# Moving a precomputed weight combination of a seven-product encoder layer from its merge to its first projections, and giving paired weight loads a second set of buffers

## The chip, the cores and the metric

The kernel is one program on one core of one Trainium2 chip. A core has TensorE for matmuls (PE in the profile, with its weight loads as PEld), VectorE (DVE), ScalarE (ACT), GpSimd (POOL) and SyncE (SP). SP computes nothing here: it issues most of the DMA transfers. Every engine works through its own queue in order, and waits on semaphores for the others. The metric is the device time of one execution in microseconds (us).

## The reference

One layer of an encoder runs over two sequences, 256 and 1024 tokens of width 1024, in float32. The kernel treats them as 1280 tokens, that is ten tiles of 128. Cut to its stages:

```
h      = rms_norm(x);  proj = h @ w_in                     # z, conv channels, gates, q, k, v, ...
b0..b3 = ssd_mixer, pool_mixer, sgu_mixer, gla_mixer       # four branches, 512 wide
merged = sum_n sigmoid(gate_n) * (b_n @ w_branch[n])       # "the merge"
x      = x + rms_norm(merged @ w_out)
hidden = relu(rms_norm(x) @ w_ff1) ** 2                    # first product, 1024 to 4096
out    = x + rms_norm(hidden @ w_ff2)                      # second product, 4096 to 1024
```

The SSD mixer comes first. Its input, 768 channels, goes through a depthwise convolution over five tokens and a SiLU before its scans.

## The kernel before, in words

**Numbers.** Each float32 operand is split into a high and a low part (`whi` and `wlo` for weights), and a product takes three passes (high-high, high-low, low-high) at 128x128 weights by up to 512 columns. For a weight block of 128x512 (256 KB) this takes a load into a buffer `raw`, a copy by ACT to `whi` and a subtraction by DVE to `wlo` (`wload`, L129 to L137). There are three buffers of the tag `raw` and sixteen of the tag `w`.

**Seven products in place of eight.** Some of the gate projections and most of both feed-forward products use a scheme of the Strassen-Winograd kind: a 2x2 block product is made with seven block products over sums and differences of blocks. On the weights' side these are T1 = B12 - B11, T2 = B22 - T1, T3 = B22 - B12 and T4 = B21 - T2. For the second product the seven are done one after another (`SECOND`), each over 5 pairs of token tiles and 4 groups of 4 weight blocks. Before product i+1 needs its 16 weight blocks, they are loaded and split while product i runs (`ff2_w`, L1351 to L1367). The right sides T1, T3 and T4 need two blocks each (`RIGHT`): both are loaded into buffers of the tag `raw`, and one DVE subtraction (L1360) makes the difference in the first of them. T4 takes T2 as its second block.

**T2 made ahead.** T2 of the second product needs three blocks and is used twice (as itself and in T4). It is therefore made once, in 16 pieces of 128x512, and kept in DRAM (`t2d`). In the kernel before this happens during the merge: `t2_in(q)` loads B12, B11 and B22 of piece q through POOL's DMA queue (L1093, the tiles named `B` in the profile) and `t2_out(q)` makes two DVE subtractions (L1098, L1099) and stores the piece through POOL's queue (L1100). The buffers are a pool of their own, two of each of the three. The code allows a new piece from step 3 of the merge's 32 steps on, one every 13/8 steps, so the last one at step 27, counted from 0; a piece goes out one step after it came in.

**The merge** (L1103 to L1134) takes 32 steps, eight blocks of 128 output channels for each of four branches, in the order 0, 2, 1, 3. A step makes three products (256, 512 and 512 tokens, each 12 matmuls, L1125) in four PSUM banks of the tag `mm`. DVE takes each out of PSUM: for the first branch one operation (L1130, into `merged`), for the others two (L1132, L1133). `branch` (L1064 to L1073) loads the four 128x1280 pieces of a branch (`bt`) and splits them by ACT (L1071) and DVE (L1072), the first branch through POOL's DMA queue, the others through SP's. Each step also needs one gate tile (`gate`, 640 KB) and one weight block.

**The front.** After the input norm and transposes, PE makes the z projection (L172, to about 77 us), the small `misc` projection and the six projections of the SSD mixer's channels (`conv_gemm`, L453 to L463, 94 to 183 us), each three chunks of 256, 512 and 512 tokens with 24 matmuls. The convolution of each, on DVE, takes one operation (L549), four (L552), a tanh by ACT (L554) and one more (L555), all 1284 elements wide. Then PE runs 11 us of other projections (`fill(11)`; `fill` puts in pieces of later projections) before it transposes the convolved channels (`token_major`, L585). `chunk_state` and the loop behind it use tiles `sx`, `xst` and `rtmp` of the pool `sv`.

**What sets the order.** From the SSD stage on, PE's order is that of the code (`manual_schedule` for PE). The other engines' queues, those of the DMA issuers too, are ordered by a scheduler when the program is built, so an instruction can stand in its queue well ahead of its place in the code. An engine never leaves that order at run time. A tile waits for the last use of the memory that it takes over.

Of the kernel before, what the change touches and what calls it, by code (L numbers as in the profile page):

```python
# [8 lines left out]
F32 = mybir.dt.float32  # L9
# [3 lines left out]
ALU = mybir.AluOpType  # L13
# [9 lines left out]
DFF = 4096  # L23
# [53 lines left out]
FF2_U = FF1_U + 64  # L77
# [4 lines left out]
def encoder_kernel(ctx, tc, x, wu, small, rows, w2, sguw, poolw, consts, y):  # L82
    nc = tc.nc
    PS = bass.MemoryType.PSUM
    PE, ACT, DVE, POOL, SP = nc.tensor, nc.scalar, nc.vector, nc.gpsimd, nc.sync

    def pool(name, bufs=1, **kw):
        return tc.alloc_tile_pool(name=name, bufs=bufs, reuse_waits="tile", **kw)

    dram = ctx.enter_context(tc.tile_pool(name="dram", bufs=1, space=bass.MemoryType.DRAM))  # L90
    cp = pool("const")
    wp = pool("w")
# [4 lines left out]
    def mm_ps():  # L97
        return pmm.tile([128, 512], F32, tag="mm", name="mm", bufs=4)
# [62 lines left out]
    def gemm_a(ps, w, act, c, n):  # L161
        j, last = 0, 3 * w.nk - 1
        for k in range(w.nk):
            for a, b in PASSES:
                PE.matmul(ps[:, :n], w.get(a, k), act.rhs(b, k, c), start=j == 0, stop=j == last)
                j += 1
# [83 lines left out]
    def ts():  # L250
        return tp.tile([128, 512], F32, tag="ts", name="ts", bufs=3)
# [104 lines left out]
    def scratch(name, n):  # L356
        return [dram.tile([128, 512], F32, name=f"{name}{i}") for i in range(n)]
# [22 lines left out]
    def gelu2(ps, n):  # L380

        a = ev1("ga")
        ACT.activation(out=a[:, :n], in_=ps[:, :n], func=AF.Square, scale=float(np.sqrt(0.044715)))
        DVE.scalar_tensor_tensor(out=a[:, :n], in0=a[:, :n], scalar=1.0, in1=ps[:, :n], op0=ALU.add, op1=ALU.mult)
        ACT.activation(out=a[:, :n], in_=a[:, :n], func=AF.Tanh, scale=float(np.sqrt(2.0 / np.pi)))
        DVE.scalar_tensor_tensor(out=a[:, :n], in0=a[:, :n], scalar=1.0, in1=ps[:, :n], op0=ALU.add, op1=ALU.mult)
        return a
# [21 lines left out]
    for g in range(4):  # L409
        tasks.append((stream_a, WA, SU_U + 2 * g, lambda ps, c, c0, n, d=sud[g]: SP.dma_start(  # L410
            out=d[:, c0:c0 + n], in_=gelu2(ps, n)[:, :n])))
    for n_b in EARLY:
        for q in range(8):
            tasks.append((stream_a, WA, GATE_U + 16 * n_b + 2 * q, lambda ps, c, c0, n, d=gtd[n_b][q]: ACT.dma_start(
                out=d[:, c0:c0 + n], in_=tanh_half(ps, n)[:, :n])))
# [13 lines left out]
    def fill(us):  # L429

        while us > 0:
# [2 lines left out]
                return  # L434
            us -= cost

    w = WB(Z_U, 8, given=zw)
    for t in range(NT):
        ps = mm_ps()
# [11 lines left out]
    sv = pool("sv")  # L451

    def conv_gemm(i):  # L453
        w = WA(XBC_U + 2 * i, 8)
        pad = sv.tile([128, NTOK + 8], F32, name="pad", bufs=2)
        for a, b in ((0, 2), (258, 262), (1286, 1288)):
            POOL.memset(pad[:, a:b], 0.0)
        for c, (c0, n) in enumerate(CH):
            ps = mm_ps()
            gemm_a(ps, w, hT, c, n)  # L460
            o = 2 + c0 if c == 0 else 6 + c0
            ACT.copy(out=pad[:, o:o + n], in_=ps[:, :n])
        return pad  # L463
# [24 lines left out]
    for d in range(2):  # L488
        DVE.tensor_tensor(out=dtx[:, d], in0=tp[:, :160].rearrange("p (t e h) -> p e t h", t=NT, e=2)[:, d],
                          in1=smv("dt_bias")[:, 8 * d:8 * d + 8].unsqueeze(1).to_broadcast([128, NT, 8]), op=ALU.add)  # L490
# [13 lines left out]
    for d in range(2):  # L504
        DVE.scalar_tensor_tensor(out=dtx[:, d], in0=dt[:, d], scalar=-1.0,
                                 in1=ea[:, 8 * d:8 * d + 8].unsqueeze(1).to_broadcast([128, NT, 8]),
# [14 lines left out]
    for g in range(2):  # L521
        ACT.activation(out=dec[64 * g:64 * g + 64].rearrange("p d t h -> p (d t) h"),
                       in_=ps[64 * g:64 * g + 64, 160:320].rearrange("p (q h) -> p q h", h=8)[:, :, 4 * g:4 * g + 4],
# [53 lines left out]
    def v4(a):  # L577
        return a.rearrange("p (h q) -> p h q", h=4)

    xsd = scratch("xsd", NT)  # L580

    def token_major(t):
# [494 lines left out]
        SP.dma_start(out=th, in_=gtd[n][d])  # L1077
        return th


    t2p = pool("t2", side="right")
    t2d = [dram.tile([128, 512], F32, name=f"t2d{q}") for q in range(DFF // 256)]

    def w2_block(b, q):
        if b == "T2":
            return t2d[q]
        return wu[FF2_U + 2 * (2 * q + int(b[1]) - 1) + int(b[2]) - 1]

    def t2_in(q):
        r = []  # L1090
        for b in ("B12", "B11", "B22"):
            r.append(t2p.tile([128, 512], F32, tag=b, name=b, bufs=2))
            POOL.dma_start(out=r[-1], in_=w2_block(b, q))  # L1093
        return r

    def t2_out(q, r):
        b12, b11, b22 = r
        DVE.tensor_tensor(out=b12, in0=b12, in1=b11, op=ALU.subtract)  # L1098
        DVE.tensor_tensor(out=b22, in0=b22, in1=b12, op=ALU.subtract)  # L1099
        POOL.dma_start(out=t2d[q], in_=b22)  # L1100

    t2q = []
    MERGE = [(n, d) for n in ORDER for d in range(8)]  # L1103
    br = branch(ORDER[0], POOL, CH)
    wb = WA(BR_U + 8 * MERGE[0][0] + MERGE[0][1], 4)
# [1 line left out]
    for i, (n_b, d) in enumerate(MERGE):  # L1107
        if i + 1 < len(MERGE):
            nwb = WA(BR_U + 8 * MERGE[i + 1][0] + MERGE[i + 1][1], 4)
        if i + 2 < len(MERGE):  # L1110
            ths.append(gate_in(*MERGE[i + 2]))
        if d == 0 and i:
            br = branch(n_b, SP, ((0, NTOK),))
        if t2q and t2q[-1] is not None:
            t2_out(len(t2q) - 1, t2q[-1])
            t2q[-1] = None
        if len(t2q) < DFF // 256 and i >= 3 + len(t2q) * 13 // 8:
            t2q.append(t2_in(len(t2q)))
        th = ths.pop(0)
        for c, (c0, n) in enumerate(CH):  # L1120
            ps = mm_ps()
            j = 0
            for k in range(4):
                for a, b in PASSES:
                    PE.matmul(ps[:, :n], wb.get(a, k), br[b][k][:, c0:c0 + n], start=j == 0, stop=j == 11)  # L1125
                    j += 1
            dst = merged[:, d, c0:c0 + n]
            t = th[:, c0:c0 + n]
            if i < 8:
                DVE.scalar_tensor_tensor(out=dst, in0=t, scalar=1.0, in1=ps[:, :n], op0=ALU.add, op1=ALU.mult)  # L1130
            else:
                DVE.scalar_tensor_tensor(out=t, in0=t, scalar=1.0, in1=ps[:, :n], op0=ALU.add, op1=ALU.mult)  # L1132
                DVE.tensor_tensor(out=dst, in0=dst, in1=t, op=ALU.add)  # L1133
        wb = nwb  # L1134
    gt.release()
    t2p.release()


    tp = pool("tp")
# [1 line left out]
    op = pool("op", side="right")  # L1141
# [209 lines left out]
    def ff2_w(i, upto):  # L1351

        while len(ws[i]) < upto:
            g, k = divmod(len(ws[i]), 4)
            raw = []
            for b in RIGHT[SECOND[i][1]]:
                raw.append(wp.tile([128, 512], F32, tag="raw", name="raw", bufs=3))
                SP.dma_start(out=raw[-1], in_=w2_block(b, 4 * GO[g] + k))
            if len(raw) > 1:
                DVE.tensor_tensor(out=raw[0], in0=raw[0], in1=raw[1], op=ALU.subtract)  # L1360
            place = (NG * i + g) % 7
            pl, tag, n = (w2p, "w2", 16) if place < 2 else (wp, "w", 16) if place < 4 else (w3p, "w3", 24)
            hi = pl.tile([128, 512], F32R, tag=tag, name="whi", bufs=n)
            lo = pl.tile([128, 512], F32R, tag=tag, name="wlo", bufs=n)
            ACT.copy(out=hi, in_=raw[0])  # L1365
            DVE.tensor_tensor(out=lo, in0=raw[0], in1=hi.bitcast(F32), op=ALU.subtract)  # L1366
            ws[i].append((hi, lo))  # L1367
# [187 lines left out]
```

## Time and profile before

| | us |
|---|---|
| median of three timed runs | 2244.68 |
| their range | 2243.88 to 2245.01 |
| the profiled execution's own time | 2240.51 |
| its span | 2238.4 |
| PE busy | 2171.2 |
| DVE busy | 1389.2 |
| ACT busy | 883.2 |
| POOL busy | 99.6 |

The profile is of one execution. Its span runs from the first to the last instruction; the 2.1 us between span and time lie around it. Busy time counts what an engine does, not what it waits for. Matmuls overlap in the profile (each row's duration holds its pipeline), so the number of matmuls in a stretch says more of PE's pace than its busy time. A row of the timeline has start and duration in us, engine, line, operation, the tile written and the tiles read, how many, and in brackets the idle time before it and what ended that. A row of the waits has who waited for whom, then the total in us, how often, and the longest. A row of the windows has the stretch and its length, then each engine's busy time with its number of instructions, the granted TensorE clock, the busy share of the DMA engines and their GB/s.

### The profile page before, as it was taken

Reading aid. Unit: us, or ns where it says so; the run is one execution under the profiler, and the core shown is the slowest. Engines: PE = TensorE matmul, PEld = TensorE weight load, DVE = VectorE, ACT = ScalarE, POOL = GpSimd, SP = SyncE. Lnnn points to the kernel's source line nnn. Section 1 sums busy time; section 2 is a strip of 40 time slices with the busy share of each in tenths; the row PEclk is TensorE's granted clock in tenths of the full one; section 3 lists DMA queues with packets and bytes.
Section 4 is the critical chain, followed back from the end, with each engine's and each line's share of the span. In section 5 each row is a group of like instructions: output and inputs, shape, how many; then the busy total and the mean of one; then the engine's idle time right before and its main releaser. Section 6 shows DMA issues by size and latency. Waiting matters only on the chain. (4 is left out here: it accounts for less than half of the span.)

```text
span 2238.4 us, 33108 instructions
## 1 busy us (share of the span) xinstructions
PE 2171.2 (97%) x12160; PEld 1917.7 (86%) x12160; DVE 1389.2 (62%) x2374; ACT 883.2 (39%) x1811; POOL 99.6 (4%) x194
## 2 busy tenths in 40 slices
PE   8999999999999999998889999999999999999998
PEld 6887888878888999997668877899999998888776
DVE  6365489677668744444466556576666684466574
ACT  5323787334333444444111124443333354333342
POOL 1000000000010000001310001000000000000000
PEclk9999999999999999998899999999999999999998
DMA  5212465545257333336885322655445577577684
GB/s 184 80 33 102 153 230 168 171 138 164 86 177 223 95 94 93 104 96 197 304 305 179 133 92 100 214 148 150 124 133 151 163 228 227 175 223 234 200 275 136
DMA packets 274866, 362.77 MB, mean 162 GB/s; under 512 B 21616, under 2 KB 160272, under 8 KB 274704
## 3 DMA queue, kind: packets, MB, share of 16 engines
q1 hardware_dynamic: 259216, 325.52, 46.7%
q0 software_dynamic: 5696, 19.40, 2.5%
q10 hardware_dynamic: 9792, 15.73, 2.0%
q8 instruction: 95, 1.56, 0.3%
q14 instruction: 67, 0.55, 0.1%
HBM read 250.92 MB, written 109.66 MB: 161 GB/s over the span
## 5 line engine op out<-in xcount | busy, mean ns | idle before, releaser
L345 PE MATMUL mm<-hT,whi 128*128 128x512 f32 (+1 forms) x960 | 261.6, 361 | 0.0
L1125 PE MATMUL mm<-bt,whi 128*128 128x512 f32 (+1 forms) x768 | 212.8, 365 | 29.2 <-DVE merged L1130 17.4
L1433 PE MATMUL mm<-whi,hidh 128*128 128x512 f32 x560 | 219.4, 392 | 2.5 <-ACT whi L1365 2.5
L1433 PE MATMUL mm<-whi,hidl 128*128 128x512 f32 x560 | 219.3, 392 | 1.9 <-DVE hidl L1375 1.9
L1433 PE MATMUL mm<-wlo,hidh 128*128 128x512 f32 x560 | 219.0, 391 | 0.6 <-DVE wlo L1366 0.6
L135 ACT CAST whi<-raw 128x512 fp32r<-128x512 f32 x142 | 87.1, 620 | 261.3 <-PE mm L1125 171.6
L345 PEld LDWEIGHTS mm<-hT,whi 128*128 128x128 f32 x960 | 166.9, 189 | 26.4 <-issue 3.3
L1125 PEld LDWEIGHTS mm<-bt,whi 128*128 128x128 f32 x768 | 139.3, 194 | 56.1 <-DVE merged L1130 20.2
L345 PE MATMUL mm<-hT,wlo 128*128 128x512 f32 (+1 forms) x480 | 170.3, 355 | 0.0
L311 PE MATMUL mx<-S,whi 128*128 128x256 f32 (+1 forms) x768 | 166.2, 308 | 0.0
L311 PE MATMUL mm<-S,whi 128*128 128x384 f32 (+1 forms) x704 | 157.5, 313 | 2.3 <-ACT fc L315 2.3
L352 PE MATMUL mm<-whi,hT 128*128 128x512 f32 x480 | 152.2, 398 | 0.0
L1125 PE MATMUL mm<-bt,wlo 128*128 128x512 f32 (+1 forms) x384 | 138.3, 360 | 0.0
L136 DVE TENSOR_TENSOR wlo<-raw,whi 128x512 fp32r<-128x512 f32 x142 | 97.0, 687 | 65.6 <-ACT whi L135 65.1
L1365 ACT CAST whi<-raw 128x512 fp32r<-128x512 f32 x112 | 69.1, 621 | 166.7 <-DVE raw L1360 112.9
L268 ACT CAST whi<-ts 128x512 fp32r<-128x512 f32 x112 | 69.2, 621 | 161.3 <-PE mm L311 78.7
L311 PEld LDWEIGHTS mx<-S,whi 128*128 128x128 f32 x768 | 128.8, 189 | 0.0
L1433 PEld LDWEIGHTS mm<-whi,hidh 128*128 128x128 f32 x560 | 105.8, 189 | 25.6 <-ACT whi L1365 3.3
L1433 PEld LDWEIGHTS mm<-whi,hidl 128*128 128x128 f32 x560 | 105.8, 189 | 25.2 <-DVE hidl L1375 3.5
L269 DVE TENSOR_TENSOR wlo<-ts,whi 128x512 fp32r<-128x512 f32 x112 | 77.1, 689 | 80.6 <-ACT whi L268 80.4
L1433 PEld LDWEIGHTS mm<-wlo,hidh 128*128 128x128 f32 x560 | 105.6, 189 | 23.0 <-DVE wlo L1366 1.2
L311 PE MATMUL mm<-hT,whi 128*128 128x256 f32 (+1 forms) x576 | 124.7, 308 | 0.0
(331 smaller groups left out, 4899.1 us busy)
## 6 DMA issues: line engine op xcount, KB each, us to landing
raw<-in_wu_dram SPq DMA_DIRECT2D x362, 256.0 KB, 3.0
gate<-gtd SPq DMA_DIRECT2D x32, 640.0 KB, 4.9
hraw<-hidS SPq DMA_DIRECT2D x80, 256.0 KB, 3.2
hraw<-hidA SPq DMA_DIRECT2D x60, 256.0 KB, 3.3
B<-in_wu_dram POOLq DMA_DIRECT2D x48, 256.0 KB, 5.4
hidS<-fc SPq DMA_DIRECT2D x64, 192.0 KB, 3.2
E<-acsd SPq DMA_DIRECT2D x20, 512.0 KB, 4.7
br<-bo SPq DMA_DIRECT2D x36, 256.0 KB, 3.0
```

Of the source, the lines that this page charges most:

```text
L135: ACT.copy(out=hi, in_=raw)
L136: DVE.tensor_tensor(out=lo, in0=raw, in1=hi.bitcast(F32), op=ALU.subtract)
L268: ACT.copy(out=hi, in_=a)
L269: DVE.tensor_tensor(out=lo, in0=a, in1=hi.bitcast(F32), op=ALU.subtract)
L311: PE.matmul(ps, w[ro][a][:, 128 * k:128 * k + 128], left(lo, p, k, c), start=first and j == 0, stop=j == 11, skip_group_check=not first)
L345: yield from halves(ps, w, n, lambda ps, w, a, b, k, st, sp: PE.matmul(ps[:, :n], w.get(a, k), hT.rhs(b, k, c), start=st, stop=sp))
L352: yield from halves(ps, w, 512, lambda ps, w, a, b, k, st, sp: PE.matmul(ps, hT.lhs(b, k, t), w.get(a, k), start=st, stop=sp))
L1125: PE.matmul(ps[:, :n], wb.get(a, k), br[b][k][:, c0:c0 + n], start=j == 0, stop=j == 11)
L1365: ACT.copy(out=hi, in_=raw[0])
L1433: PE.matmul(ps, h[b][:, 128 * k:128 * k + 128], ws[i][4 * g + k][a], start=g == 0 and k == 0 and (a, b) == (0, 0), stop=g == NG - 1 and k ...
```

## The change

- The making of T2 moves to the front. `t2_step` is called after each of the 18 chunks of `conv_gemm`: it finishes the piece that is loaded and begins the next one, so 17 calls make all 16. A loop ahead of `token_major` would finish what is left.
- Its loads and stores go through SP's queue instead of POOL's.
- Its buffers are now tiles of the pool `sv` that are used only later: `sx` for B12 (one buffer), `rtmp` for B11 (one, now 128x512 wide) and `xst` for B22 (two). The pool `t2` is gone.
- In `ff2_w`, the second block of T1, T3 and T4 is loaded into a buffer of the tag `ts` (three of them, which are idle in the second product); the first stays in `raw`.

The operations of T2, their sizes and their number are the same as before.

```diff
+    def t2_in(q):
+        r = []
+        for b, tag in (("B12", "sx"), ("B11", "rtmp"), ("B22", "xst")):
+            r.append(sv.tile([128, 512], F32, tag=tag, name=tag, bufs=2 if tag == "xst" else 1))
+            SP.dma_start(out=r[-1], in_=w2_block(b, q))
+        return r
+
+    def t2_out(q, r):
+        b12, b11, b22 = r
+        DVE.tensor_tensor(out=b12, in0=b12, in1=b11, op=ALU.subtract)
+        DVE.tensor_tensor(out=b22, in0=b22, in1=b12, op=ALU.subtract)
+        SP.dma_start(out=t2d[q], in_=b22)
+
+    def t2_step():
+        if t2q and t2q[-1] is not None:
+            t2_out(len(t2q) - 1, t2q[-1])
+            t2q[-1] = None
+        if len(t2q) < DFF // 256:
+            t2q.append(t2_in(len(t2q)))
...
             gemm_a(ps, w, hT, c, n)
+            t2_step()
             o = 2 + c0 if c == 0 else 6 + c0
...
+    while len(t2q) < DFF // 256 or t2q[-1] is not None:
+        t2_step()
     xsd = scratch("xsd", NT)
...
-    t2p = pool("t2", side="right")
...
-            r.append(t2p.tile([128, 512], F32, tag=b, name=b, bufs=2))
-            POOL.dma_start(out=r[-1], in_=w2_block(b, q))
...
-        POOL.dma_start(out=t2d[q], in_=b22)
...
-        if t2q and t2q[-1] is not None:
-            t2_out(len(t2q) - 1, t2q[-1])
-            t2q[-1] = None
-        if len(t2q) < DFF // 256 and i >= 3 + len(t2q) * 13 // 8:
-            t2q.append(t2_in(len(t2q)))
...
             for b in RIGHT[SECOND[i][1]]:
-                raw.append(wp.tile([128, 512], F32, tag="raw", name="raw", bufs=3))
+                raw.append(ts() if raw else wp.tile([128, 512], F32, tag="raw", name="raw", bufs=3))
                 SP.dma_start(out=raw[-1], in_=w2_block(b, 4 * GO[g] + k))
```

More of the change, by code (lines that the diff above doesn't have):

```diff
@@ L435, in fill, with w2_block @@
             us -= cost
+    t2d = [dram.tile([128, 512], F32, name=f"t2d{q}") for q in range(DFF // 256)]
+    def w2_block(b, q):
+        if b == "T2":
+            return t2d[q]
+        return wu[FF2_U + 2 * (2 * q + int(b[1]) - 1) + int(b[2]) - 1]
+    def t2_in(q):
[9 more added lines that the diff above has]
+        SP.dma_start(out=t2d[q], in_=b22)
+    t2q = []
+    def t2_step():
[4 more added lines that the diff above has]
+            t2q.append(t2_in(len(t2q)))
     w = WB(Z_U, 8, given=zw)
@@ L1078, in gate_in @@
         return th
-    t2p = pool("t2", side="right")
[L1082 to L1091, printed above, removed]
-            r.append(t2p.tile([128, 512], F32, tag=b, name=b, bufs=2))
[L1093 to L1102, printed above, removed]
     MERGE = [(n, d) for n in ORDER for d in range(8)]
@@ L1135, in encoder_kernel @@
     gt.release()
-    t2p.release()
     tp = pool("tp")
```

## The prediction

> **What bounds the kernel now.** I read the page first, then who waits for whom on PE, then windows of the stages in which PE waits.
>
> ```profile
> span 2238.4 us, 33108 instructions
> PE 2171.2 (97%) x12160; PEld 1917.7 (86%) x12160; DVE 1389.2 (62%) x2374; ACT 883.2 (39%) x1811; POOL 99.6 (4%) x194
> PEclk9999999999999999998899999999999999999998
> ```
>
> PE is the bound: 97% of the span, and its clock is down only in slices 19, 20 and the last. So work moved on other engines counts only where PE waits.
>
> ```profile
> PE mm L1125 <- DVE merged L1130: 17.4, 10, 3.3
> PE mm L1125 <- ACT bt L1071: 10.7, 4, 7.1
> ...
> PE mm L1433 <- ACT whi L1365: 2.5, 2, 2.1
> ```
>
> The largest waits are those of the merge (L1125): for DVE to take a product out of PSUM, and at the start for the first branch's tiles. The second product (L1433) waits little. Busy time understates the loss, because a matmul at a lower clock counts as busy. I count matmuls instead:
>
> ```profile
> core 0: us, PE busy (x) PEld busy (x) DVE busy (x) ACT busy (x) POOL busy (x), PEclk, DMA share, GB/s
> 1045.50:1061.20 15.70, 5.01 (x15) 3.26 (x14) 8.79 (x15) 6.79 (x14) 3.99 (x8) 0.66 1.02 371
> 1061.20:1080.00 18.80, 15.48 (x59) 12.39 (x59) 8.80 (x13) 5.48 (x5) 3.85 (x9) 0.77 0.95 369
> 1080.00:1155.00 75.00, 60.28 (x289) 48.90 (x289) 39.36 (x63) 8.67 (x11) 25.41 (x47) 0.97 0.84 294
> 1155.00:1170.00 15.00, 14.49 (x75) 12.14 (x74) 13.73 (x22) 2.41 (x3) 0.00 (x0) 1.00 0.90 306
> 1170.00:1300.00 130.00, 130.00 (x681) 112.00 (x680) 82.49 (x138) 17.58 (x24) 0.00 (x0) 1.00 0.43 149
> ```
>
> From 1170 us on PE is never idle: 130 / 681 = 0.191 us per matmul. At that pace the four stretches before would take 2.9, 11.3, 55.2 and 14.3 us. They lose 12.8, 7.5, 19.8 and 0.7 us, together 40.8. POOL is busy in the first three only, and POOL does nothing there but issue DMAs, nearly all for T2.
>
> **Part 1: T2 leaves the merge.** The long stretch shows how T2 costs PE time:
>
> ```profile
> 1099.49 0.69 DVE L1099 TENSOR_TENSOR B<-B,B 128x512 f32<-128x512 f32 x1 [4.41 <-DMA B<-in_wu_dram]
> 1100.10 0.68 DVE L1130 SCALAR_TENSOR_TENSOR merged<-gate,mm 128x512 f32<-128x512 f32 x1
> 1101.88 0.69 DVE L1098 TENSOR_TENSOR B<-B,B 128x512 f32<-128x512 f32 x1 [1.09 <-DMA B<-in_wu_dram]
> 1102.49 0.68 DVE L1130 SCALAR_TENSOR_TENSOR merged<-gate,mm 128x512 f32<-128x512 f32 x1
> ```
>
> A subtraction stands in DVE's queue ahead of an evacuation and waits 4.41 us for its block. The evacuation behind it starts at once when it is through. PE has four banks and stops when all are full. DVE's work is not too much (39.4 of 75 us); its order is the trouble. Without the 32 subtractions each step of the first branch leaves DVE three evacuations and one split. What then remains is at most what the stretch from 1155 us loses, where DVE works at 13.7 of 15 us without T2, 0.7 us. I leave 1 and take 18.8 of the 19.8; the lower bound is the idle time alone, 75 - 60.3 = 14.7.
>
> The Trainium skill's "TensorE: Matmul & The Clock Gate", Part 1, says that PE drops to half its clock after an idle window of about 3.4 us and needs as long a busy one to return. The clock of 0.66 and 0.77 behind the 7.1 us wait agrees, and so does 0.97 in the long stretch, where no wait passed 3.3 us. By that rule the long stretch loses only 14.7 us and 3% of 60, 16.5 together, and the forecast would be about 2.3 us later.
>
> The start of the merge:
>
> ```profile
> 1031.77 0.72 POOL L1093 DMA_DIRECT2D B<-in_wu_dram  x1 [325.94 <-PE mm L311]
> 1042.48 2.16 POOL L1093 DMA_DIRECT2D B<-in_wu_dram  x4 [9.99 <-PE mx L311]
> 1044.63 2.24 POOL L1067 DMA_DIRECT2D bt<-br  x4
> ...
> 1149.80 0.54 POOL L1100 DMA_DIRECT2D t2d<-B  x1 [3.76 <-DVE B L1099]
> ```
>
> Four T2 blocks go out right ahead of the first branch's tiles. That costs 2.16 us of issue, and 1.0 MB at the 371 GB/s of that stretch, where the DMA engines are full (1.02), is 2.8 us more. Some later T2 blocks share the same time. I take 6 us; the bounds are 2.2 (the issue alone) and 10.7 (the whole wait). The second half of those tiles overwrites what the gates' last product still reads, so a wait stays. In the second stretch the second branch's tiles come next over the same DMA engines: I take 1.5 of 7.5, bounds 0 and 7.5. The merge: 18.8 + 6 + 1.5 = 26.3, say 26, with 17 to 33 as the span that I believe (the sum of the lower ends is 16.9; all upper ends at once would need both start waits gone).
>
> **Part 2: T2 in the front.** It brings 32 subtractions of 0.69 us, 22 us of DVE, 48 loads and 16 stores of 256 KB on SP. The rows above also say when it will run: its first block was issued at 1031.77 us, before the merge began, and its last store at 1149.80, in step 10 (by 1155 us PE had made 363 matmuls, at 36 a step), though the code allows the last piece at step 27. Queues other than PE's are filled with what is ready. In the front the same is seen:
>
> ```profile
> 40.01 0.17 POOL L457 MEMSET pad<- 128x2 f32 x3
> ```
>
> This memset belongs to the first `conv_gemm` and to the pool whose tiles T2 will use, and it ran while PE was still at the z projection. So T2 starts at about 41 us, far ahead of the chunks in which it is written.
>
> ```profile
> 40.00:75.00 35.00, 35.00 (x164) 29.15 (x163) 9.21 (x14) 7.73 (x15) 0.18 (x4) 1.00 0.14 51
> 75.00:108.00 33.00, 32.39 (x177) 27.74 (x176) 12.21 (x24) 12.74 (x24) 0.17 (x3) 1.00 0.31 99
> 108.00:140.00 32.00, 32.00 (x181) 27.97 (x181) 19.13 (x18) 11.21 (x22) 0.34 (x6) 1.00 0.10 32
> 140.00:195.00 55.00, 55.00 (x289) 47.46 (x288) 40.56 (x34) 16.62 (x26) 0.34 (x6) 1.00 0.18 56
> ```
>
> ```profile
> raw<-in_wu_dram SPq DMA_DIRECT2D x362, 256.0 KB, 3.0
> B<-in_wu_dram POOLq DMA_DIRECT2D x48, 256.0 KB, 5.4
> ```
>
> With one buffer for B12 the pieces run one after another: store and three loads issued, the last one landed, two subtractions. With SP's 3.0 us and no time for issue that is 4.4 us a piece, with POOL's 0.54 us an issue it is 6.5; I take 5.3, 85 us for 16, from 41 to 126 us (bounds 70 and 105 us). From 40 to 140 us DVE has 59 us idle against 22 needed, and the DMAs carry 32 to 99 GB/s; T2 adds 16.8 MB in 85 us, 197 GB/s, and 371 were seen. SP's other transfers there are the z stores and weight loads several projections ahead; behind a T2 load that waits for DVE they come a few us late, under chunks of 5 us in four banks. What the cover hides must end in time here:
>
> ```profile
> 193.89 1.50 DVE L555 SCALAR_TENSOR_TENSOR xcm<-pad,xcm 128x1284 f32<-128x1284 f32 x1 [0.80 <-ACT pad L554]
> ```
>
> ```profile
> 195.82 0.60 PE L585 MATMUL mx<-cst,xcm 128*128 128x128 f32 x4
> ```
>
> The last convolution ends at 195.39 us and PE reads it at 195.82. There is 0.43 us of slack: any lateness of DVE at that point is PE's. But lateness from T2 up to 126 us meets an idle stretch first:
>
> ```profile
> 139.96 0.69 DVE L136 TENSOR_TENSOR wlo<-raw,whi 128x512 fp32r<-128x512 f32 x1 [7.10 <-ACT whi L135]
> ```
>
> The 7.1 us before it take it up. I charge 1 us, with 0 and 8 as the likely ends; a gain is excluded, since PE waits for nothing here that T2 could relieve.
>
> **Part 3: buffers for the second blocks.**
>
> ```profile
> 1838.00:2060.00 222.00, 222.00 (x981) 183.80 (x981) 124.35 (x192) 86.61 (x152) 0.00 (x0) 1.00 0.68 215
> 2060.00:2090.00 30.00, 28.12 (x120) 21.80 (x119) 19.62 (x32) 14.43 (x26) 0.00 (x0) 1.00 0.72 222
> 2170.00:2190.00 20.00, 16.90 (x61) 12.85 (x60) 14.82 (x27) 7.84 (x17) 1.41 (x2) 0.83 0.77 257
> ```
>
> ```profile
> 2171.76 0.70 DVE raw L1360
> 2172.48 3.93 DMA raw<-t2d
> 2176.50 0.69 DVE raw L1360
> ```
>
> Undisturbed, the second product takes 222 / 981 = 0.226 us per matmul. Where T1 and T4 are first needed it loses 30 - 27.2 = 2.8 and 20 - 13.8 = 6.2 us, together 9.0. The chain shows why: a second block starts only when the subtraction before it has freed its buffer, and this pair takes 4.7 us, while PE uses a weight block in 2.7 (12 of its matmuls). With three buffers for first and three for second blocks, three pairs are under way. Then ACT and DVE are late next (DVE is busy 14.8 of those 20 us), so I take 7, bounds 0 and 9. It adds no instruction.
>
> **Sum.** 26 + 7 - 1 = 32 us: the profiled execution goes from 2240.5 to 2208.5. It was 4.2 us under the median of the runs, so the median goes from 2244.7 to 2212.7.
>
> **The rivals.**
>
> *T2 holds up the convolutions (slower).* If T2 runs inside the projections as written, its subtractions stand in DVE's queue between the convolutions and wait there for blocks, as in the merge:
>
> ```profile
> DVE B L1099 <- DMA B<-in_wu_dram: 18.4, 5, 4.4
> DVE B L1098 <- DMA B<-in_wu_dram: 12.8, 7, 3.7
> ```
>
> That is 31.2 / 16 = 1.95 us of waiting and 1.38 of work a piece, 53 us for 16. From 108 to 195 us DVE has 27.3 us idle. If none of it can be used, because those gaps are waits for PE, PE is 53 us late at 195.82: 2244.7 - 33 + 53 = 2265. It turns slower from 33 us, 2.1 us a piece. If all of the idle is used, 25.7 us stay: 2237.4. Against it speaks the early order above. 7% and 9%.
>
> *Blocks land no faster on SP.* The 5.4 us of the B loads may come from the full DMA engines (0.84 to 1.02) or from POOL's queue. If a block takes 5.4 us on SP as well, a piece takes 9.0 us and T2 ends at 185. Five pieces then fall behind 140 us, 16.7 us of DVE against 14.4 idle: 2 to 17 us late, about 2222. For it: the same engines move the blocks. Against it: in the front they are busy 0.10 to 0.31. The Trainium skill's "DMA: Bandwidth & Descriptors", "Issuing engines are not separate DMA queues", says that the issuing engine changes only the sequencer's time, which would make this the case wherever the load is equal; no run shows equal load yet. 9%.
>
> *The second product gains nothing*, since casts and not buffers are late there (L1365 is what PE names): 2219.7. 15%.
>
> **Chances.** The forecast has 58%; 2% is for a stage that I do not see. A measurement of this kernel can tell about 0.2%, 4.5 us, from no change. Faster: 58 + 15 + 9 and most of the 9 of the mild delay, 0.87; same 0.05; slower 0.08. The range runs from 33 + 9 - 0 = 42 us gained, 2203, to 17 + 3 - 7 = 13, 2232; outside it lie the late convolutions.
>
> **What would show it.** Right: no T2 load after 200 us, the first near 41, the last store by 146; L1130 with no DMA wait ahead of it, and the merge's 289 matmuls of the long stretch in about 56 us; first split of `bt` some 6 us sooner after the gates' last product; 0.226 us per matmul through T1 and T4; the transposes (L585) where they were, within 2 us. Wrong: a wait of PE for `xcm` of more than a few us, a merge that still loses over 20 us, or DVE's L1360 still waiting for its second block.

## The result and the profile after

| | before | changed |
|---|---|---|
| median, us | 2244.85 | 2206.70 |
| range of its runs, us | 2243.88 to 2245.78 (4) | 2204.60 to 2207.95 (4) |
| the profiled execution's time, us | 2240.51 | 2204.60 |
| its span, us | 2238.4 | 2202.8 |

The ratio is 0.9829, with a 95% interval of 0.9812 to 0.9846: the changed kernel is faster by 38.2 us, where the forecast was 32. Two later sets, each beside the kernel before, gave 30.3 and 34.6 us (the last part of the experiments).

From here on lines of the changed kernel have its own numbers: the merge's matmul L1125 is now L1130, its evacuations L1130, L1132 and L1133 are L1135, L1137 and L1138, the branch's splits L1071 and L1072 are L1104 and L1105, T2's subtractions are L454 and L455, the second product's L1360, L1365 and L1433 are L1364, L1369 and L1437, and the transposes of the convolved channels (L585) are L618.

The page of the changed kernel, its head:

```profile
span 2202.8 us, 33087 instructions
PE 2164.1 (98%) x12160; PEld 1917.6 (87%) x12160; DVE 1389.5 (63%) x2374; ACT 883.9 (40%) x1811; POOL 64.5 (3%) x130
PEclk9999999999999999999999999999999999999999
```

PE has as many matmuls as before and is 7.1 us less busy, in a span 35.6 us shorter. The rest of the gain is idle time. Who waits for whom on PE, changed kernel (total, times, longest):

```profile
PE mx L196 <- DVE xn L232: 9.5, 3, 7.8
PE mm L1130 <- ACT bt L1104: 5.6, 4, 3.6
PE mm L311 <- ACT fc L315: 3.7, 4, 1.1
```

The 17.4 us for `merged` are gone, the wait for the first branch has halved, and no wait of the second product (L1437) is left. The windows of the changed kernel, cut close to where the windows of the kernel before were cut (13, 70, 358 and 432 matmuls of the merge had started at their ends there, 15, 73, 360 and 433 here; the first begins at the end of the gates' last product):

```profile
core 0: us, PE busy (x) PEld busy (x) DVE busy (x) ACT busy (x) POOL busy (x), PEclk, DMA share, GB/s
1048.15:1059.60 11.45, 5.47 (x16) 3.65 (x16) 7.47 (x14) 6.44 (x14) 1.06 (x2) 0.61 1.05 410
1059.60:1072.10 12.50, 12.50 (x60) 10.51 (x59) 5.29 (x8) 5.41 (x5) 0.00 (x0) 0.95 0.85 338
1072.10:1127.10 55.00, 55.00 (x289) 47.36 (x288) 30.22 (x44) 9.86 (x13) 0.00 (x0) 1.00 0.60 216
1127.10:1141.10 14.00, 14.00 (x75) 12.04 (x74) 8.33 (x15) 1.28 (x3) 0.00 (x0) 1.00 0.43 132
1814.00:2036.00 222.00, 222.00 (x981) 183.80 (x980) 129.78 (x202) 92.34 (x160) 0.00 (x0) 1.00 0.72 226
2036.00:2194.90 158.90, 158.90 (x702) 131.28 (x700) 100.33 (x172) 60.88 (x119) 5.48 (x9) 1.00 0.65 208
```

Cut at exactly the same matmuls, by their starts in the two traces, the merge reads:

| stretch of the merge | before, us | changed, us | gained, us |
|---|---|---|---|
| end of the gates' last product to the merge's 16th matmul (the start) | 16.8 | 11.8 | 5.0 |
| the next 59 matmuls (the second stretch) | 19.0 | 12.3 | 6.6 |
| the next 289 (the long stretch) | 74.4 | 55.3 | 19.1 |
| the next 75 | 15.0 | 14.2 | 0.8 |
| the rest | 137.3 | 137.3 | 0.0 |

The 289 matmuls now go at 0.191 us each, PE's own pace. In the second product all go at 0.226 us.

Where the span's 35.6 us come from is read by the time at which the same instruction starts in the two traces:

| | before, us | changed, us | difference |
|---|---|---|---|
| first transpose of the convolved channels | 195.8 | 198.0 | +2.2 |
| end of the gates' last product | 1045.7 | 1048.2 | +2.5 |
| first matmul of the output projection (the merge's end) | 1308.1 | 1279.1 | -29.0 |
| first matmul of the first product | 1426.7 | 1398.0 | -28.7 |
| end of its plain part (L1301, now L1305) | 1480.8 | 1454.4 | -26.4 |
| first matmul of the second product | 1838.0 | 1814.0 | -24.0 |
| end of its last matmul | 2228.8 | 2194.9 | -33.9 |
| end of the span | 2238.4 | 2202.8 | -35.6 |

The front lost 2.2 us, the merge gained 31.5, about 5 were given back between merge and second product, the second product gained about 10 and the end of the span 1.7.

### The profile page after: what moved, and what is told of

It is laid out like the page before. It is cut to its first block, busy times and chain, and to the rows that moved or that the text cites. A ratio compares the mean times of both kernels' runs of the same rounds, so it can differ in the third digit from the quotient of the medians.

```text
span 2202.8 us, 33087 instructions
## 1 busy us (share of the span) xinstructions
PE 2164.1 (98%) x12160; PEld 1917.6 (87%) x12160; DVE 1389.5 (63%) x2374; ACT 883.9 (40%) x1811; POOL 64.5 (3%) x130
## 5 line engine op out<-in xcount | busy, mean ns | idle before, releaser
L1437 PE MATMUL mm<-wlo,hidh 128*128 128x512 f32 x560 | 217.9, 389 | 0.0
L1437 PE MATMUL mm<-whi,hidl 128*128 128x512 f32 x560 | 217.9, 389 | 0.0
L1437 PE MATMUL mm<-whi,hidh 128*128 128x512 f32 x560 | 217.8, 389 | 0.0
L1130 PE MATMUL mm<-bt,whi 128*128 128x512 f32 (+1 forms) x768 | 207.8, 358 | 6.0 <-ACT bt L1104 5.6
L135 ACT CAST whi<-raw 128x512 fp32r<-128x512 f32 x142 | 86.9, 620 | 244.3 <-PE mm L1130 163.0
L1130 PEld LDWEIGHTS mm<-bt,whi 128*128 128x128 f32 x768 | 137.4, 191 | 28.5 <-ACT bt L1104 6.8
L1378 ACT CAST hidh<-hraw 128x512 fp32r<-128x512 f32 x140 | 86.4, 620 | 128.4 <-PE mm L1437 115.6
L1379 DVE TENSOR_TENSOR hidl<-hraw,hidh 128x512 fp32r<-128x512 f32 x140 | 95.7, 689 | 66.6 <-ACT hidh L1378 66.0
L1130 PE MATMUL mm<-bt,wlo 128*128 128x512 f32 (+1 forms) x384 | 136.5, 355 | 0.0
L1437 PEld LDWEIGHTS mm<-whi,hidh 128*128 128x128 f32 x560 | 105.1, 188 | 22.0
L311 PEld LDWEIGHTS mm<-S,whi 128*128 128x128 f32 x704 | 119.4, 189 | 5.4 <-ACT fc L315 5.4
L1437 PEld LDWEIGHTS mm<-whi,hidl 128*128 128x128 f32 x560 | 105.1, 188 | 21.7
```

The lines of the kernel that those rows point to most:

```text
L135: ACT.copy(out=hi, in_=raw)
L311: PE.matmul(ps, w[ro][a][:, 128 * k:128 * k + 128], left(lo, p, k, c), start=first and j == 0, stop=j == 11, skip_group_check=not first)
L1378: ACT.copy(out=hh, in_=raw)
L1379: DVE.tensor_tensor(out=hl, in0=raw, in1=hh.bitcast(F32), op=ALU.subtract)
L1437: PE.matmul(ps, h[b][:, 128 * k:128 * k + 128], ws[i][4 * g + k][a], start=g == 0 and k == 0 and (a, b) == (0, 0), stop=g == NG - 1 and k ...
```

## The experiments

**The theory:** T2 cost the merge its time because its subtractions stood in DVE's queue ahead of the evacuations and waited there for blocks; in the front they wait as well, but nothing that PE needs stands behind. The second product is a gain of its own. **The rivals:** T2's traffic, 16.8 MB, is what held up the merge, wherever the subtractions run; or DVE had too much work; or the buffers only looked useful because everything else moved.

Each experiment ran beside the kernel before. Three sets were run, and the kernel before took 2240.21 us (e1 to e4), 2234.35 (e5 to e8) and 2239.76 (e9 to e11), so an experiment is compared with its own set.

### The two halves apart (e1, e2)

e1 is the changed kernel with the second blocks back in `raw`:

```diff
-                raw.append(ts() if raw else wp.tile([128, 512], F32, tag="raw", name="raw", bufs=3))
+                raw.append(wp.tile([128, 512], F32, tag="raw", name="raw", bufs=3))
```

> T2 is made in the front as in the changed kernel, and the second blocks of T1, T3 and T4 stay in the three-deep raw ring as in the kernel before. Theory (two separate gains: about 30 us from the merge, about 10 us from the second product's buffers; the traces gave 31.5 and 9.7): 2216 us (2213 to 2220), L364-type subtraction on VectorE again waiting about 113 us in all ahead of the hi copy, and matmuls of the second product waiting near 9 us. Rival (the second product only gained because the front or the merge ended earlier or at another phase): 2207, within 2 us of the changed kernel.

Measured: 2211.16 us, ratio 0.9871 (0.9855 to 0.9887), 29.1 us under the kernel before. e2 is the kernel before with the buffers alone, T2 still in the merge:

```diff
-                raw.append(wp.tile([128, 512], F32, tag="raw", name="raw", bufs=3))
+                raw.append(ts() if raw else wp.tile([128, 512], F32, tag="raw", name="raw", bufs=3))
```

> T2 stays in the merge as in the kernel before; only the second blocks of T1, T3 and T4 go to buffers of their own. Theory: 2235 us (2232 to 2238), nothing changed up to the merge's end, 9.7 us gained in the second product. Rival (the buffers gain nothing by themselves): 2244 to 2246.

Measured: 2234.65 us, ratio 0.9972 (0.9961 to 0.9982), 5.6 us under. The two add to 34.6 us, as much as the whole change gained beside e9 and e10 and between the 38.2 and 30.3 us of its two other sets. So they are separate, and the buffers do gain by themselves. The sizes were off: e1 came out 5 us quicker than expected, and its second product is 6 us quicker than in the trace of before. The window of e2 over the whole second product, T2's place unchanged:

```profile
1841.20:2222.10 380.90, 380.90 (x1681) 315.10 (x1679) 230.37 (x374) 153.50 (x278) 5.50 (x9) 1.00 0.68 218
```

It takes 381 us without a stop, as in the changed kernel. With the second blocks in `raw` it took 390.8 us in the trace of before, but 384.7 in e1, 387.6 in e3, 385.2 in e5 and 387.5 in e9; with buffers of their own 381.0 to 381.2 in all eight traces. The ring of three `raw` buffers costs 4 to 10 us from one execution to the next, and the trace of before was the worst of them. In e1 ACT waits for the subtractions as long as before (the wait of L1369 for L1364 is 112.2 us, against 112.9), yet PE waits only 2.6 us in all.

### The subtractions off DVE, then the block on SP gone (e3, e5)

e3 is the kernel before with one edit:

```diff
-        DVE.tensor_tensor(out=b12, in0=b12, in1=b11, op=ALU.subtract)
-        DVE.tensor_tensor(out=b22, in0=b22, in1=b12, op=ALU.subtract)
+        POOL.tensor_tensor(out=b12, in0=b12, in1=b11, op=ALU.subtract)
+        POOL.tensor_tensor(out=b22, in0=b22, in1=b12, op=ALU.subtract)
```

> The kernel before with one edit: T2's two subtractions run on GpSimd in place of VectorE; their 48 loads and 16 stores stay in the merge, on the same queue. Theory (the long stretch of the merge was lost because the evacuations stood behind T2's subtractions in VectorE's queue, and these waited for their blocks): the matmuls of the merge no longer wait for the DVE merged evacuations, 16 to 22 us gained, 2226 us (2222 to 2230); the wait at the merge's start stays. Rival (T2's 16 MB of traffic in the merge is what held up gates and branch, whoever subtracts): 2241 to 2247, the waits staying in another name.

Measured: 2233.1 us, ratio 0.9968 (0.9955 to 0.9981): 7 us under, which fits neither. The windows of e3, in the same cuts, and the two slices behind them:

```profile
1063.80:1077.80 14.00, 13.46 (x60) 10.79 (x59) 5.59 (x7) 4.22 (x4) 6.22 (x9) 0.91 1.02 406
1077.80:1135.00 57.20, 55.49 (x288) 47.25 (x287) 30.61 (x41) 9.93 (x13) 35.52 (x45) 1.00 0.89 313
1155.00:1175.00 20.00, 10.39 (x58) 8.87 (x56) 1.86 (x3) 0.00 (x0) 11.77 (x15) 0.84 0.64 205
1175.00:1195.00 20.00, 16.66 (x76) 14.13 (x77) 13.39 (x24) 2.49 (x4) 0.00 (x0) 0.81 0.87 319
```

The long stretch is back at 57.2 us for 288 matmuls, with all of T2's traffic in it (DMA engines 0.89 busy). But from 1155 to 1195 us PE made 134 matmuls where 212 were possible. The waits of SP in e3's merge and the row in ACT's timeline show a second queue behind T2:

```profile
SPq L1211 <- DMA B<-in_wu_dram: 28.8, 2, 24.3
```

```profile
1176.01 0.62 ACT L135 CAST whi<-raw 128x512 fp32r<-128x512 f32 x1 [25.41 <-DMA raw<-in_wu_dram]
```

L1211 loads `oxt` for the output projection. Its tile takes over memory of T2's blocks, so it waits until POOL is through with them, and in SP's queue it stands ahead of the merge's next weights. In the kernel before the same order is there and costs nothing: SP came to this load at 1157.7 us, when T2's last store had already gone out (1149.8). e5 is e3 with `oxt` loaded from POOL's queue:

```diff
     def residual(t, ps):
         xt = op.tile([128, D], F32, name="oxt", bufs=2)
-        SP.dma_start(out=xt, in_=x[t * 128:(t + 1) * 128, :])
+        POOL.dma_start(out=xt, in_=x[t * 128:(t + 1) * 128, :])
```

> The kernel before with T2's subtractions on GpSimd, as in the experiment before this one, and the ten loads of oxt for the output projection issued from GpSimd in place of SyncE. In the trace of that experiment the matmuls ran without a gap between 1095 and 1135 us, and the two stretches 1155 to 1195 held 134 matmuls where two full ones hold 212; SyncE waited there 24.3 us in one piece at the oxt load, which lies in the space of T2's blocks and stood ahead of the merge's own weights. Theory (two queues stood behind T2, VectorE's and SyncE's; the traffic itself costs little): the 78 missing matmuls come back, about 14 us, so 19 to 24 us under the kernel before (2217 to 2222 if that is again at 2240), matmuls of the merge waiting under 15 us in all and mostly at its start. Rival (T2's traffic is what costs, and the stall only changes its name): 5 to 10 us under the kernel before.

Measured: 2213.07 us, ratio 0.9908 (0.9894 to 0.9923), 21.3 us under, as expected. The merge's windows in e5:

```profile
1043.70:1060.70 17.00, 6.09 (x15) 4.24 (x16) 8.05 (x13) 6.60 (x14) 8.36 (x11) 0.63 1.03 386
1060.70:1074.50 13.80, 12.47 (x58) 10.21 (x57) 5.49 (x7) 4.29 (x5) 7.46 (x9) 0.96 0.98 389
1074.50:1130.30 55.80, 55.14 (x287) 46.97 (x286) 30.55 (x41) 9.61 (x13) 34.08 (x45) 1.00 0.90 317
```

All 64 transfers of T2 are still here. Cut at the same matmuls the long stretch takes 56.6 us, nearly PE's pace, next to DMA engines that are 0.90 busy, which ends the rival of the traffic there; the second stretch takes 14.1, and only the start (17.0 us against 16.8) has stayed.

### Work or waiting (e9)

e9 leaves the subtractions on DVE and takes the waiting away: the blocks are loaded once, and every piece subtracts the same three.

```diff
-        r = []
-        for b in ("B12", "B11", "B22"):
-            r.append(t2p.tile([128, 512], F32, tag=b, name=b, bufs=2))
-            POOL.dma_start(out=r[-1], in_=w2_block(b, q))
-        return r
+        if q == 0:
+            for b in ("B12", "B11", "B22"):
+                t2k.append(t2p.tile([128, 512], F32, tag=b, name=b, bufs=1))
+                POOL.dma_start(out=t2k[-1], in_=w2_block(b, q))
+        return t2k
...
-        DVE.tensor_tensor(out=b12, in0=b12, in1=b11, op=ALU.subtract)
-        DVE.tensor_tensor(out=b22, in0=b22, in1=b12, op=ALU.subtract)
-        POOL.dma_start(out=t2d[q], in_=b22)
+        d = t2p.tile([128, 512], F32, tag="d", name="d", bufs=1)
+        o = t2p.tile([128, 512], F32, tag="o", name="o", bufs=2)
+        DVE.tensor_tensor(out=d, in0=b12, in1=b11, op=ALU.subtract)
+        DVE.tensor_tensor(out=o, in0=b22, in1=d, op=ALU.subtract)
+        POOL.dma_start(out=t2d[q], in_=o)
...
+    t2k = []
```

> The kernel before with T2's subtractions left on VectorE in the merge, 32 as before, and its 16 stores too, but its blocks are loaded once, for the first piece, and the 15 others subtract the same three blocks again, so that nothing waits for a load (45 of the 48 loads and 15 of the 16 true values of T2 are left out; the second product takes what was stored). Theory (the evacuations were late because the subtractions ahead of them waited for blocks, 34 us in the trace of before, not because of the 20 us that the subtractions themselves take): the merge, 255 us in the trace of before and 230 in the changed kernel's, takes 230 to 238, and with the loads gone from its start too it is 20 to 27 us under the kernel before. Rival (VectorE's own work is what was too much): the merge still takes 247 to 255, at most 10 us under the kernel before.

Measured: 2211.5 us, ratio 0.9869 (0.9855 to 0.9882), 28.3 us under, about one more than the theory's 27; the merge took 233.8 us. Its windows:

```profile
1045.20:1057.50 12.30, 5.91 (x16) 3.92 (x16) 9.27 (x17) 6.66 (x14) 2.16 (x4) 0.58 1.04 397
1071.00:1129.70 58.70, 56.14 (x289) 47.35 (x288) 41.21 (x65) 10.40 (x14) 6.47 (x12) 1.00 0.72 260
```

The long stretch takes 58.8 us with DVE busy for 41.2 of them. Of the 19 us that it lost, about 16 were waiting and 3 to 4 the subtractions' own time. e9 takes most of T2's loads out along with the waiting; that their traffic costs little in this stretch is what e5 shows, where all of it stays. And with the loads gone the merge's 16th matmul starts 12.7 us after the gates' last product where it was 16.8: the 4.1 us between are the price of the blocks ahead of the first branch.

### T2 left in the merge, with nothing behind it (e10)

e10 is e5 with the buffers of the second product:

```diff
-                raw.append(wp.tile([128, 512], F32, tag="raw", name="raw", bufs=3))
+                raw.append(ts() if raw else wp.tile([128, 512], F32, tag="raw", name="raw", bufs=3))
```

> T2 stays in the merge with its subtractions on GpSimd and oxt loaded from there (the kernel that was 21 us under the kernel before), and the second blocks of T1, T3 and T4 have buffers of their own. Theory (the gains are separate and add): second product at 381 us in place of 385, so 4 to 6 us under that kernel, 25 to 28 under the kernel before, and 3 to 6 us over the changed kernel, all of it at the merge's start, where T2's first loads stand ahead of the branch's. Rival (the place makes no difference once no queue stands behind T2): within 2 us of the changed kernel.

Measured: 2210.20 us, ratio 0.9869 (0.9856 to 0.9883), 29.6 us under the kernel before, a little more than expected, and 5.1 us over the changed kernel in the same set. In the traces it needs 239.3 us from the gates' last product to the merge's end, the changed kernel of that set 231.7. Of the 7.6 us between them 4.6 lie at the merge's start, as expected, and 2.0 in the long stretch (57.4 against 55.3). So most of what the move brought can be had without moving T2.

### What T2 costs in the front (e4, e7, e8)

e4 is the changed kernel without T2:

```diff
             gemm_a(ps, w, hT, c, n)
-            t2_step()
...
-    while len(t2q) < DFF // 256 or t2q[-1] is not None:
-        t2_step()
...
         if b == "T2":
-            return t2d[q]
+            b = "B22"
```

> The changed kernel with T2 left out altogether: no load, subtraction or store of it, and the second product takes B22 in the place of T2, so that the same number of blocks is loaded there. Theory (T2 in the front costs what the traces show up to the transposes, 2.2 us): 2204.5 us, 1 to 4 us under the changed kernel. First rival (it costs nothing, the 2.2 us were of the single execution): within 1 us of the changed kernel. Second rival (it costs the 4.9 us lost later between the merge and the first product too): 2199 to 2201.

Measured: 2202.38 us, ratio 0.9832 (0.9819 to 0.9845). The changed kernel did not run in this set; it had 0.9829, 0.9868 and 0.9838 in its own three (2206.7, 2204.0 and 2205.1 us). By the times T2 in the front costs 2 to 4 us, by two of the ratios about 1 us or nothing; the runs tell no more than between nothing and 4 us. The traces say about the same: without T2 the transposes start at 195.5 us, with it at 198.0, 195.7 and 198.4 in three executions. In the two that lose over 2 us, PE waits 0.9 and 1.5 us ahead of the small transposes of `dtr` (L517) and its clock is 0.83 and 0.85 in the 10 us from 95 us on; in the third, and in the kernel before, the wait is 0.6 us and the clock 1.00. The window and the waits of the changed kernel:

```profile
75.00:108.00 33.00, 31.73 (x162) 27.01 (x161) 17.03 (x32) 11.58 (x21) 0.17 (x3) 0.95 0.77 245
```

```profile
PE mx L517 <- ACT dtr L503: 0.9, 1, 0.9
DVE sx L454 <- DMA sx<-in_wu_dram: 32.2, 12, 4.1
```

DVE waits 32 us for T2's blocks here, about as long as in the merge, where by e5 PE lost some 18 us by it in the long stretch (74.4 to 56.6). e7 has T2's loads and stores in the front on POOL's queue:

```diff
-            SP.dma_start(out=r[-1], in_=w2_block(b, q))
+            POOL.dma_start(out=r[-1], in_=w2_block(b, q))
...
-        SP.dma_start(out=t2d[q], in_=b22)
+        POOL.dma_start(out=t2d[q], in_=b22)
```

> The changed kernel with T2's loads and stores issued by GpSimd in place of SyncE; the subtractions stay on VectorE. Theory (in the front T2 is hidden by idle engines on any queue, and weights' loads on SyncE only get shorter): within 2 us of the changed kernel, blocks landing in 4 to 5 us in place of 3.2, T2's last store between 150 and 185 us. Rival (the descriptors that GpSimd makes are slow, its queue stands behind the memsets of pad, and T2 goes past the transposes near 196): 4 to 20 us slower than the changed kernel.

Measured: 2213.43 us, ratio 0.9909 (0.9894 to 0.9924), 9.4 us over the changed kernel in the same set, which is the rival's size, but not its reason: the last store goes out at 152.3 us, well ahead of 196. The loads' landing times in the front, changed kernel and then e7:

```profile
sx<-in_wu_dram SPq DMA_DIRECT2D x16, 256.0 KB, 3.7
rtmp<-in_wu_dram SPq DMA_DIRECT2D x16, 256.0 KB, 2.9
```

```profile
sx<-in_wu_dram POOLq DMA_DIRECT2D x16, 256.0 KB, 4.0
rtmp<-in_wu_dram POOLq DMA_DIRECT2D x16, 256.0 KB, 2.9
```

At equal load the queues are alike. What the trace shows of the 10 us are waits of PE for `dtr` (2.6 us), for a weight's lo part (2.0) and for a convolved channel (2.8), and a clock of 0.90 between 75 and 108 us; the transposes start at 205.9. The order made when the program is built differs too: one piece more stands ahead of the evacuations of `misc` (L506) in DVE's queue, and the subtraction right ahead of one of them (96.51 us) waits 3.85 us for its block. That this is what makes `dtr` and the lo part late is likely, but it was not tried apart.

e8 has T2's subtractions in the front on POOL:

```diff
-        DVE.tensor_tensor(out=b12, in0=b12, in1=b11, op=ALU.subtract)
-        DVE.tensor_tensor(out=b22, in0=b22, in1=b12, op=ALU.subtract)
+        POOL.tensor_tensor(out=b12, in0=b12, in1=b11, op=ALU.subtract)
+        POOL.tensor_tensor(out=b22, in0=b22, in1=b12, op=ALU.subtract)
```

> The changed kernel with T2's two subtractions in the front on GpSimd in place of VectorE; loads and stores stay on SyncE. Theory (the 2.2 us that the front lost come from subtractions ahead of weights' lo parts and of the dtr evacuation in VectorE's queue: a later transposition of dtr and then half a slice at a granted clock of 0.83): transposes at 195.5 to 196.5 us in place of 198.0, 1 to 2.5 us under the changed kernel. First rival (SyncE's queue and the traffic did it, 234 GB/s where 52 stood): as the changed kernel. Second rival (the memsets of pad stand behind subtractions that wait, and the convolutions come late): 3 to 15 us slower.

Measured: 2206.51 us, ratio 0.9876 (0.9859 to 0.9893), 2.5 us over the changed kernel, within the intervals of both. The theory's half about `dtr` held (PE waits 0.6 us there, as in the kernel before), but a new wait came, that of the second rival, just under its lower end. Waits of PE and ACT in e8:

```profile
PE mm L165 <- ACT pad L493: 3.0, 1, 3.0
ACT pad L493 <- POOL xst L455: 2.6, 1, 2.6
```

The memset of a new `pad` stood behind subtractions in POOL's queue. The transposes start at 200.9 us.

### The changed kernel again (e6, e11)

> The changed kernel once more, beside these. Theory: 38 us under the kernel before (35 to 40), the second product again at 381 us without a matmul waiting, the front again 1 to 3 us later at the transposes than the kernel without T2 (195.5 us), the first product's 54 us again lengthened by about 2. Rival (what was lost between the merge and the second product belonged to the one execution): that part back at 54.

Measured: 2204.03 us, ratio 0.9868 (0.9849 to 0.9886), 30.3 us under the kernel before in place of 38. The front lost nothing in this execution. The plain part of the first product took 56.3 us again.

> The changed kernel a third time, beside the two others. It was 38 us under the kernel before in one set and 30 in the next, where the kernel before took 2244.9 and 2234.4 us and itself 2206.7 and 2204.0. Theory (the kernel before waits for blocks 34 us in the merge, so its time follows how fast blocks land on the chip at hand; the changed kernel waits for hardly any): 2203 to 2208 whatever the kernel before takes this time. Rival (the whole chip was quicker in the second set): the two move together.

Measured: 2205.12 us, ratio 0.9838 (0.9825 to 0.9852), 34.6 us under. Over the three sets the changed kernel stays within 2.7 us (2206.7, 2204.0, 2205.1) while the kernel before ranges over 10.5 (2244.9, 2234.4, 2239.8; 2240.2 in the set of e1 to e4). The three sets stand in the same order for both, so a quicker set may account for 2.7 of the 10.5 us at most; the gain is 30 to 38 us because the kernel before varies more. The two sets at 2240.2 and 2239.8 us ran on one chip and that at 2234.4 on another, so the chip may have a part in it. That the waits for blocks make the kernel before vary fits the spread of the second product (385 to 391 us in `raw`, 381 without), but it was not profiled in the set at 2234 us, so this is argued and not shown.

## Why the prediction was right, step by step

**The bound, and counting matmuls.** Right. The long stretch was to gain 18.8 us, by its count of matmuls; it went from 74.4 to 55.3 us, 19.1. The clock rule's 16.5 us (the Trainium skill, "TensorE: Matmul & The Clock Gate", Part 1) was too little: the clock of 0.97 and the idle time together do not hold all that short waits cost. Part of the 0.97 is a fall behind a wait of 3.1 us (the clock is 0.71 from 1110 to 1115 us).

**DVE's order, not its work.** Right for the long stretch, shown by e9 (waiting 16, work 3 to 4) and e5 (the pace returns once the subtractions leave DVE's queue). What the prediction did not see is that SP's queue stood behind T2 as well, through memory that `oxt` takes over. It cost nothing in the kernel before and did not touch the sum; it cost e3 its gain.

**The start of the merge.** 6 us forecast. It went from 16.8 to 11.8, 5.0 us; e9, with T2's loads left out in the old place, gives 4.1.

**The second stretch: the step that failed.** The prediction took 1.5 of 7.5 us, since "in the second stretch the second branch's tiles come next over the same DMA engines". The 59 matmuls went from 19.0 us to 12.3, a gain of 6.6: the term was 5.1 us too small. What PE waited for is seen in DVE's timeline, the kernel before and then the changed one:

```profile
1073.64 1.49 DVE L1072 TENSOR_TENSOR bt<-bt,bt 128x1280 fp32r<-128x1280 f32 x1 [9.48 <-ACT bt L1071]
1075.05 0.68 DVE L1130 SCALAR_TENSOR_TENSOR merged<-gate,mm 128x512 f32<-128x512 f32 x1
```

```profile
1067.67 1.49 DVE L1105 TENSOR_TENSOR bt<-bt,bt 128x1280 fp32r<-128x1280 f32 x1 [4.31 <-ACT bt L1104]
```

A split of the second branch's first tile stands in DVE's queue ahead of an evacuation and waits 9.5 us for that tile, whose cast by ACT starts 26.7 us after the gates' last product (18.2 in the changed kernel). Behind it PE stopped for 3.3 us, its longest wait for an evacuation, and then ran at half its clock (0.50 from 1075 to 1080 us). In the changed kernel the split waits 4.3 us and PE does not stop. So the late tiles that the prediction named are what PE stopped behind, and their price was mis-sized: they cost by a wait and again by the clock behind it, about 3.3 us each. e5 does not speak against it: with the subtractions on GpSimd 7 of T2's transfers land between the gates' last product and the tile, where 10 did, the cast starts at 24.6 us, PE's longest wait for an evacuation there is 1.3 us, the clock stays at 0.96, and the 59 matmuls take 14.1 us. How much of these 4.9 us is the tile's and how much the order's was not tried apart.

**T2 in the front.** Its start near 41 us was right (first load at 40.1, as the memset had shown). The piece of 5.3 us was too short: the last store was issued at 148.6 us, 6.8 us a piece, because DVE waited 32 us for blocks (141.9 in e6, 6.4 a piece). The bound of 6.5 for a piece was nearly the truth, and the sign "last store by 146" was missed by 2.6 us. The cost, 1 us with 0 and 8 as ends, was 2.2 in the profiled execution, then -0.1 and 2.6. It was sought at the slack of 0.43 us; it arose at `dtr`, 100 us earlier, most of it as a lower clock (0.83 over 10 us is 1.7 us). The idle 7.1 us near 140 were not needed in the way forecast: DVE waits less for weights there (the waits of L136 in the first 200 us went from 35.4 to 9.2 us) and the convolutions ended 2.2 us late, no more.

**The second product.** 7 of 9.0 forecast; 9.8 from the trace of before to that of the changed kernel (390.8 to 381.0), 5.6 (4.0 to 8.7, from the interval) by e2's runs, 4 in the traces of e5 and e10. The mechanism was right: PE waits there no more, and ACT and DVE are not late next, as was feared. The 9.0 were read from an execution in which the ring did badly, so that the profiled gain came out near them is luck.

**What the sum lacked.** About 5 us were given back between merge and second product, 2 of them in the plain part of the first product (below) and 2.4 behind it, in the part up to the second product; and 1.7 us were gained at the end of the span. Neither had a term. The part up to the second product took 357.2 to 358.1 us in the five traces with the second blocks in `raw` and 358.4 to 360.5 in the eight with buffers of their own; PE waits there 2.8 to 3.4 us in all in the five and 3.4 to 5.2 in the eight, mostly for `fc` from ACT (L315). So the new buffers seem to cost 1 to 2 us ahead of the product that they help; why is not shown. The profiled execution gained 35.9 us where 32 stood: 5.1 more in the second stretch, 2.8 in the second product, 1.7 at the end, 0.8 in the 75 matmuls behind the long stretch and 0.3 in it, less 1.0 at the merge's start, 1.2 in the front and the 5 given back. That the total came within 4 us is thus partly luck: errors of about 11 us one way and 7 the other. The range's lower end, too, was added up from 3 and 7 us where the bounds given before were 0 and 8; with these it is 9 us gained and not 13, and the result lies inside either way.

**The rivals.** That T2 holds up the convolutions did not happen: in three executions of the changed kernel the transposes behind them came between 0.1 us sooner and 2.6 us later. Blocks on SP did land sooner than POOL's 5.4 us, but e7 shows that it was not the queue: on either queue `sx` takes 3.7 to 4.0 us and `rtmp` 2.9 where the load is the same. That agrees with the Trainium skill, "DMA: Bandwidth & Descriptors", "Issuing engines are not separate DMA queues". The prediction's number came out right since the front's DMA engines were emptier. That the second product gains nothing is ruled out by e2.

## What to carry to other kernels

An instruction that waits for a transfer costs what stands behind it in its queue, not what it does: ask of each queue, the DMA issuers' too, what stands behind and who needs it, and look for memory that a later tile takes over from the one that waits. When one such wait goes, the next queue behind the same data shows itself (e3), so the traffic is to be judged only when no queue stands behind it (e5). A stage that waits for transfers in a short ring varies by several us from run to run; a gain read from one execution of it needs a second.

## What the runs showed of the hardware

**The end of the span goes with the number of DMAs that GpSimd issued.** From the end of the last store's issue to the end of the span it takes 2.9 us in the seven traces with 4 or 23 such transfers, 4.6 in the four with 68 and 5.4 in the two with 78, whichever kernel it is. e7 differs from the changed kernel only in the queue of T2's transfers, and it has 4.6 where that has 2.9. The last stores of before and of the changed kernel:

```profile
2232.80 0.99 SPq L1422 DMA_DIRECT2D out_dram<-acc  x2
```

```profile
2198.92 0.99 SPq L1426 DMA_DIRECT2D out_dram<-acc  x2
```

The spans end at 2238.4 and 2202.8. These 1.7 us of the gain come with T2's leaving POOL's queue; what is done in that time no view shows.

**The clock can fall after a wait of about 2 us.** In the plain part of the first product PE waits once for 1.5 to 2.5 us (L1167, now L1171). In seven of the thirteen traces the granted clock is then 0.91 for a 20 us slice, and the part takes 56 to 57 us; in the other six it stays 1.00 and the part takes 54 to 55. The wait was 1.5 to 2.0 us in the six and 1.7 to 2.5 in the seven, so its length alone does not decide. The seven are the traces in which GpSimd issued 4 or 23 transfers, the six those with 68 or 78; whether the one leads to the other was not tried, and what decides is open.

**GpSimd takes 1.3 us for a subtraction that DVE does in 0.69** (128x512 float32, medians 1287 to 1295 ns in e3 and e8), and in e8 some took 2.4 to 2.6.
